# Hybrid mLSTM / gated delta-net step: weight splits scheduled ahead, and small vector work moved to GpSimd

## The chip, the cores and the metric

The kernel runs on one core of a Trainium2 chip. The metric is the device time of one execution in microseconds, from the first instruction to the last; the figure for a kernel is the median of its runs. A profiled execution gives the trace that everything below is read from.

## The reference

One inference step of a two-layer trunk on 512 prompt tokens and 8 x 4 decode tokens, all 544 handled as columns of one activation matrix of 1024 rows. Layer 0 mixes tokens with an mLSTM, layer 1 with a gated delta rule (the delta-net); each is followed by a squared-ReLU MLP of width 4096, and each sub-layer by a layer norm. The part that the change touches is the delta-net. Cut to what matters:

```
proj = x @ w_in                                  # q, k, v, z, b, a
c = silu(causal depthwise conv of width 4 over qkv, state conv0 in front)
q, k = l2norm per head;  beta = sigmoid(b);  g = -exp(a_log) * softplus(a + dt_bias)
# per token, in exact chunked form for the prompt:
S_t = e^{g_t} S_{t-1} + beta_t k_t (v_t - e^{g_t} S_{t-1}^T k_t)^T ;   o_t = S_t^T q_t
y = (head_rms(o) * norm_w * silu(z)) @ w_out
# outputs also hold the new S (8 samples x 16 heads of 128 x 128) and the last 3 conv rows
```

All matrices are fp32. A product is made from three fp32r products (high x high, low x high, high x low), so each weight tile has to be split into a high and a low part on the chip before TensorE can use it.

## The kernel before

**Weights.** Every weight is a tile of 128 x 8 x 128 values, 512 KB. `load_w` (L172) takes one of two `wraw` buffers, issues the load on SP's queue (L177), takes a buffer for the high part `wh` and one for the low part `wl` (two of each), and calls `split` (L109): ScalarE (ACT) rounds the raw tile to `wh` (L110), VectorE (DVE) writes `wl` = raw - `wh` (L111). `mm3` (L186) then issues 24 products of 272 columns on TensorE (PE) for one half of the tokens (L191), so 48 for a weight.

**Order.** The kernel is written in the Tile framework. Each engine's instructions stand in one queue, executed in order; the framework decides that order ahead of time, taking among the instructions that its plan finds ready the one that was written first. `tc.high_priority(offset=n)` makes the instructions of a block count as if written n instructions earlier. On the chip an instruction whose input is late holds everything behind it in its engine's queue.

**Delta-net (L913 on).** `ORDER` (L57) is the list of steps: `p` = `project(u)` for eight units of two heads (four weights each: k, q, v, v), `y` = `gate_out(g)` for four groups (four weights each), `w` = `out(g)` (four weights each). Between them three lanes advance in small steps: after every three products `mm3` calls `tick`, and each lane takes a step every 3 to 6 ticks (`PERIODS`, L58). The first lane holds `prepare` and `invert` (the triangular inverse of a unit's 128 x 128 chunks), the second `scan` (the chunk recurrence of the prompt), the third `decode` and `update` (the 8 x 4 decode tokens, and their states). `finish` (L165) runs the rest of a lane's work where a later step needs it.

- `conv` (L978) builds `pre` for one weight's channels: three zeros in front (L982), the conv state of the 8 samples (L983), and the projection out of PSUM (ACT, L984 to L986); copies the last rows to `cvo` for output (L988, L989); then `acc`, four taps (ACT L993, DVE L995), a sigmoid (DVE L507, ACT L508 to L510) and the product (L999, and for the samples L1002 and L1007).
- `project` copies the samples' k or q for the second head of the pair (L1033).
- `invert` uses GpSimd (POOL) for a memset and a few block copies: L1148, L1150 (scales the inverse of the 16 x 16 blocks, once it has come back through DRAM as `xc`), L1176 to L1178.
- `update` (L1403): for each of the two halves of the samples it masks the tokens' values with DVE (`VM`, L1411, two of 128 x 512), then for each of four heads fetches the state tile `st` of four samples (`sst`, four buffers, loaded three ahead by `states`), scales the keys on ACT (`KM`, L1416), issues three products of 512 columns into PSUM `pS` (L1419), and for each of the four samples DVE does state x decay + `pS` (L1424, 128 x 128). The new state is stored (L1425).

PSUM has three banks of tag g, two of a, two of s and one of t; the lanes' small products use s and a.

Of the kernel before, what the change touches and what calls it, by code (L numbers as in the profile page):

```python
# [25 lines left out]
NCH = TP // P  # L26
# [44 lines left out]
def hybrid_kernel(  # L71
# [26 lines left out]
    V, S, G, T = nc.vector, nc.scalar, nc.gpsimd, nc.tensor  # L98
    dma = nc.sync.dma_start
# [59 lines left out]
    lanes, done = [], set()  # L159
# [98 lines left out]
    bmask = cp.tile([P, NB], F32, name="bmask")  # L258
# [6 lines left out]
    with tc.tile_pool(name="tmpc", bufs=1) as tp:  # L265
# [45 lines left out]
        for i in lvl:  # L311
            w = 2 << i
# [234 lines left out]
    with tc.tile_pool(name="mc", bufs=1, reuse_waits="tile") as mc, ExitStack() as mx:  # L547
# [9 lines left out]
        with tc.tile_pool(name="mg", bufs=1, reuse_waits="tile") as mg:  # L557
# [29 lines left out]
            b = gt("b", "sp_u")  # L587
# [315 lines left out]
    with tc.tile_pool(name="gc", bufs=1, reuse_waits="tile") as gc, ExitStack() as gx:  # L903
# [63 lines left out]
        W = 3 + TP + 7 * NB  # L967
        WC = W - 3
        def samp(t):
            return t[:, 3 + TP:W].rearrange("p (b t) -> p b t", t=7)  # L970

        def tl(name, tag=None, bufs=1, n=4, dt=F32):
            return gp.tile([P, n, P], dt, tag=tag or name, name=name, bufs=bufs)

        def cv(name, n):
            return gl.tile([P, n], F32, tag="cv", name=name, bufs=NCV)

        def conv(ct, cvt, slot, dp, ds, pss):  # L978


            pre = cv("pre", W)
            V.memset(pre[:, 0:3], 0.0)  # L982
            V.tensor_copy(samp(pre)[:, :, 0:3], cvt[:, slot])  # L983
            S.copy(pre[:, 3:3 + HN], pss[0])  # L984
            S.copy(pre[:, 3 + HN:3 + TP], pss[1][:, :TP - HN])
            S.copy(samp(pre)[:, :, 3:7], pss[1][:, TP - HN:HN].rearrange("p (b t) -> p b t", t=TS))  # L986
            cvo = gp.tile([P, 27], F32, tag="cvo", name="cvo", bufs=2)
            V.tensor_copy(cvo[:, 0:3], pre[:, TP:TP + 3])  # L988
            V.tensor_copy(cvo[:, 3:27].rearrange("p (b t) -> p b t", t=3), samp(pre)[:, :, 4:7])  # L989
            dma(o_conv[:, ct, :], cvo)  # L990
            acc = cv("acc", WC)
            cw = [cst[:, C_CW + 4 * ct + q:C_CW + 4 * ct + q + 1] for q in range(4)]
            S.activation(acc, pre[:, 0:WC], AF.Copy, scale=cw[0])  # L993
            for q in range(1, 4):
                V.scalar_tensor_tensor(acc, pre[:, q:q + WC], cw[q], acc, op0=ALU.mult, op1=ALU.add)  # L995
            sgm = pre[:, 0:WC]
            sigmoid_chain(sgm, acc)
            dp = acc[:, 0:TP] if dp is None else dp
            V.tensor_tensor(dp, acc[:, 0:TP], sgm[:, 0:TP], op=ALU.mult)  # L999

            a3, s3 = acc[:, TP + 3:WC], sgm[:, TP + 3:WC]
            V.tensor_tensor(  # L1002
                ds[:, 0:7],
                a3[:, 0:49].rearrange("p (b t) -> p b t", t=7)[:, :, 0:4],
                s3[:, 0:49].rearrange("p (b t) -> p b t", t=7)[:, :, 0:4],
                op=ALU.mult)
            V.tensor_tensor(ds[:, 7], a3[:, 49:53], s3[:, 49:53], op=ALU.mult)  # L1007
            return dp, pre[:, 0:TP]

        def spare():  # L1010
# [2 lines left out]
        def project(u):  # L1013

            g, base, ct = u // 2, 12 * (u // 2) + 4 * (u % 2), 4 * u
            st = {"u": u}
            cvt = gp.tile([P, 4, NB, 3], F32, tag="cvt", name="cvt", bufs=2)
# [11 lines left out]
            for w in range(2):  # L1029
                pss = first.pop(0) if first else proj(wb[base + w])  # L1030
                xs = kqx[:, w, j0].rearrange("p (b t) -> p b t", t=TS)
                dst, sq = conv(ct + w, cvt, w, kq[:, w], xs, pss)
                V.tensor_copy(kqx[:, w, j0 + 1], kqx[:, w, j0])  # L1033
                pt = mtile("t")
                if w == 0:
                    for ch in range(NCH):
                        T.transpose(pt[:, ch * P:(ch + 1) * P], dst[:, ch * P:(ch + 1) * P], ident)
                    S.copy(ktok, pt.rearrange("p (c d) -> p c d", c=NCH))
                    for ch in range(NCH):
                        sq = gp.tile([P, P], BF16, tag="k_sq", name="k_sq", bufs=1)  # L1040
# [362 lines left out]
        def update(g, ua, ub):  # L1403

            khl, vhl = (r32(t) for t in ua["dec"])
            sts = states(g, [(h, q) for q in range(2) for h in range(4)])
            for q in range(2):
                VM = []
                for w in range(2):
                    VM.append(tl("VM", ("tok", "sx")[w], dt=F32R))  # L1410
                    V.tensor_tensor(VM[w], vhl[:, w:w + 1].to_broadcast([P, 4, P]),  # L1411
                                    bmask[:, 4 * q:4 * q + 4].unsqueeze(2).to_broadcast([P, 4, P]), op=ALU.mult)
                for h in range(4):
                    st = next(sts)
                    KM = tl("KM", ("kqs", "UAs")[h % 2], n=2, dt=F32R)
                    S.activation(KM, khl, AF.Copy, scale=blk[:, h:h + 1])  # L1416
                    pS = mtile("s").rearrange("p (b d) -> p b d", b=4)
                    for i, (a, b) in enumerate(((0, 0), (0, 1), (1, 0))):
                        T.matmul(pS, lhsT=KM[:, a], rhs=VM[b], start=(i == 0), stop=(i == 2))  # L1419
                    glc = (ua if h < 2 else ub)["glc"][:, h % 2]  # L1420
                    for r in range(4):
                        bb = 4 * q + r
                        t = st[:, r]
                        V.scalar_tensor_tensor(t, t, glc[:, NCH + bb:NCH + bb + 1], pS[:, r], op0=ALU.mult, op1=ALU.add)  # L1424
                    dma(o_ss[g, :, h, 4 * q:4 * q + 4], st)  # L1425
                    yield

# [213 lines left out]
```

## Time and profile before

| | us |
|---|---|
| median of 3 runs | 1831.82 |
| lowest and highest of the runs | 1825.68, 1838.59 |
| the profiled execution | 1825.97 |
| its span, first to last instruction | 1824.3 |
| DVE busy, of the span | 1060.5 (58%) |
| ACT busy | 827.4 (45%) |
| GpSimd busy | 55.1 (3%) |

Times in the rows are counted from the span's start. A busy PE is a modelled figure: a product's duration overlaps the next one's, so the pace of the products is read from their starts. The delta-net runs from about 710 to 1420 us.

### The profile page before, as it was taken

To read this page: it belongs to the slowest core of one execution; us is meant where nothing else is said; L and a number is where in the kernel's file an instruction comes from. 1 tells how busy PE (TensorE), PEld (TensorE's weight loads), DVE (VectorE), ACT (ScalarE), POOL (GpSimd) and SP (SyncE) were. 2 spreads that over 40 slices of the span, in tenths; PEclk is the share of its full clock that TensorE was granted. 3 is DMA by queue.
4 is the path that set the end of the run, shared out by engine and by line. 5 is a ranking of instruction groups with operands and counts; after the bars stand their busy time and mean duration, and the time that the engine had idled before them with its cause. 6 is when DMAs were issued, how large, how long until landed. Compare 5 with 4: busy or idle time off the path is not lost.

```text
span 1824.3 us, 35692 instructions
## 1 busy us (share of the span) xinstructions
PE 1755.2 (96%) x14580; PEld 1687.1 (92%) x14580; DVE 1060.5 (58%) x2648; ACT 827.4 (45%) x1874; POOL 55.1 (3%) x105
## 2 busy tenths in 40 slices
PE   7999999999999998999899999999999999999997
PEld 7999998999999998889779989998898999999996
DVE  6564767432244368776855877685578643234436
ACT  5444346331234147675643664574346542124314
POOL 2000000000000000011001000000100000000000
PEclk9999999999999999898978999997799999999998
DMA  4122222222223222223314423431232222222311
GB/s 160 58 105 64 71 93 93 71 92 87 88 93 105 82 74 61 56 50 98 111 55 122 123 68 103 130 90 41 79 121 90 90 85 93 82 93 86 111 60 50
DMA packets 84293, 158.88 MB, mean 87 GB/s; under 512 B 37537, under 2 KB 41505, under 8 KB 83617
## 3 DMA queue, kind: packets, MB, share of 16 engines
q1 hardware_dynamic: 84128, 156.60, 27.6%
q8 instruction: 115, 1.88, 0.4%
q14 instruction: 50, 0.40, 0.1%
HBM read 140.51 MB, written 16.06 MB: 86 GB/s over the span
## 4 chain that ended last, share of the span: by engine, by line
PE 81%; DVE 10%; ACT 5%; DMA 2%; issue 1%; POOL 0%; SPq 0%; ACTq 0%; DVEq 0%; POOLq 0%
PE pg_t L191 40%; PE pm_s L191 12%; PE pm_a L191 12%; PE pm_s L1368 2%; DVE lnt L377 1%; DVE lnt L378 1%; PE pm_s L1419 1%; PE pm_s L1254 1%; PE pm_a L1090 1%; PE pm_s L1265 1%; DVE acc L995 1%; ACT wh L110 1%; DVE wl L111 1%; DVE XL L389 1%; PE pm_s L1281 1%
## 5 line engine op out<-in xcount | busy, mean ns | idle before, releaser
L111 DVE TENSOR_TENSOR wl<-wraw,wh 128x1024 fp32r<-128x1024 f32 x200 | 244.7, 1224 | 360.9 <-ACT wh L110 360.3
L191 PE MATMUL pg_t<-XH,wh 128*128 128x272 f32 x1480 | 446.0, 301 | 8.7 <-ACT XH L110 7.6
L191 PE MATMUL pg_t<-XH,wl 128*128 128x272 f32 x1480 | 438.4, 297 | 7.5 <-DVE wl L111 7.5
L191 PE MATMUL pg_t<-XL,wh 128*128 128x272 f32 x1480 | 439.3, 297 | 0.1
L110 ACT CAST wh<-wraw 128x1024 fp32r<-128x1024 f32 (+1 forms) x201 | 210.4, 1047 | 465.4 <-PE pg_t L191 212.4
L191 PEld LDWEIGHTS pg_t<-XH,wh 128*128 128x128 f32 x1480 | 285.3, 193 | 13.0 <-ACT XH L110 7.6
L191 PEld LDWEIGHTS pg_t<-XH,wl 128*128 128x128 f32 x1480 | 284.5, 192 | 10.0 <-DVE wl L111 8.9
L191 PEld LDWEIGHTS pg_t<-XL,wh 128*128 128x128 f32 x1480 | 284.9, 193 | 2.4 <-DVE XL L111 0.4
L191 PE MATMUL pg_t<-h,wh 128*128 128x272 f32 x672 | 129.2, 289 | 0.0
L191 PEld LDWEIGHTS pg_t<-h,wh 128*128 128x128 f32 x672 | 105.6, 188 | 0.3
L191 PE MATMUL pg_t<-h,wl 128*128 128x272 f32 x336 | 96.9, 288 | 0.0
L191 PE MATMUL pm_a<-h,wh 128*128 128x272 f32 x496 | 95.3, 288 | 0.0
L191 PE MATMUL pm_s<-h,wh 128*128 128x272 f32 x496 | 94.9, 288 | 0.0
L191 PE MATMUL pm_s<-XH,wh 128*128 128x272 f32 x288 | 84.1, 292 | 0.0
L191 PE MATMUL pm_s<-XH,wl 128*128 128x272 f32 x288 | 83.7, 291 | 0.0
L393 DVE SCALAR_TENSOR_TENSOR XR<-XR,pg_t 128x272 f32<-128x272 f32 x118 | 51.1, 434 | 56.1 <-PE pg_t L191 55.4
L191 PE MATMUL pm_s<-XL,wh 128*128 128x272 f32 x288 | 83.7, 291 | 0.0
L191 PE MATMUL pm_a<-XL,wh 128*128 128x272 f32 x280 | 82.4, 294 | 0.9 <-DVE XL L389 0.8
L191 PE MATMUL pm_a<-XH,wh 128*128 128x272 f32 x280 | 82.9, 296 | 0.0
L191 PE MATMUL pm_a<-XH,wl 128*128 128x272 f32 x280 | 81.5, 291 | 0.0
L191 PEld LDWEIGHTS pm_s<-h,wh 128*128 128x128 f32 x496 | 77.9, 188 | 0.2
L191 PEld LDWEIGHTS pm_a<-h,wh 128*128 128x128 f32 x496 | 78.0, 188 | 0.1
(573 smaller groups left out, 3924.6 us busy)
## 6 DMA issues: line engine op xcount, KB each, us to landing
wraw<-in_w SPq DMA_DIRECT2D x64, 512.0 KB, 3.5
wraw<-in_wb SPq DMA_DIRECT2D x48, 512.0 KB, 3.5
wraw<-in_w2a SPq DMA_DIRECT2D x32, 512.0 KB, 3.5
sst<-in_s SPq DMA_DIRECT2D x64, 256.0 KB, 3.0
wraw<-in_wa SPq DMA_DIRECT2D x24, 512.0 KB, 3.5
wraw<-in_w2b SPq DMA_DIRECT2D x24, 512.0 KB, 3.4
out_ss<-sst SPq DMA_DIRECT2D x32, 256.0 KB, 3.0
wraw<-in_wbo SPq DMA_DIRECT2D x16, 512.0 KB, 3.8
```

Source lines behind the costliest of these rows:

```text
L110: S.copy(hi, src)
L111: V.tensor_tensor(lo, src, r32(hi), op=ALU.subtract)
L191: T.matmul(ps, lhsT=wt[:, k, :], rhs=xt[k][:, HS[h]], start=first and k == 0 and q == 0, stop=last and k == n - 1 and q == 2,)
L377: V.tensor_tensor(t, x, rs, op=ALU.mult)
L378: V.tensor_tensor(t, t, mu, op=ALU.subtract)
L389: V.tensor_tensor(XL[j][:, HS[h]], x, r32(XH[j][:, HS[h]]), op=ALU.subtract)
L393: V.scalar_tensor_tensor(x, x, ALPHA if first else 1.0, ps, op0=ALU.mult, op1=ALU.add)
L995: V.scalar_tensor_tensor(acc, pre[:, q:q + WC], cw[q], acc, op0=ALU.mult, op1=ALU.add)
L1090: T.matmul(pk[:, q * 256:(q + 1) * 256], lhsT=kq[:, 0, c0:c0 + P], rhs=kq[:, :, c0:c0 + P], start=True, stop=True)
L1254: T.matmul(pks[:, w], lhsT=kq[:, w, cc], rhs=St, start=True, stop=True)
L1265: T.matmul(pv[:, j], lhsT=X[:, 4 * (ch // 2) + 2 * j + ch % 2], rhs=rhs[:, j] if ch else vtok[:, j, 0], start=True, stop=True)
L1368: T.matmul(pkq[:, r], lhsT=t[:, r], rhs=kqf[:, :, o:o + 4], start=True, stop=True)
```

## The change

1. `load_w`: the load and the split of a weight stand in a block of high priority, with an offset of 300 while the lanes run (the delta-net) and 0 elsewhere; the `wh` and `wl` buffers are taken before the load is issued and not after.
2. `conv`: the two small writes to `pre` and the two to `cvo` go from DVE to GpSimd. `acc` is made as wide as `pre`, so that the samples' product is one instruction of 32 columns and not two (28 and 4). `project`: the copy of the second head goes to GpSimd.
3. `update`: the mask of the values goes from two DVE instructions of 128 x 512 to eight GpSimd instructions of 128 x 128 per half; the state is scaled by four GpSimd instructions of 128 x 128, before the products; DVE then adds `pS` to the four samples' states in one instruction of 128 x 512. After the first scaling of each half the lane gives way once more (`yield`).

```
+AHEAD = 300
 def load_w(src, alloc=None):
     raw = pool.tile([P, KD, P], F32, tag="wraw", name="wraw", bufs=WBUFS[0])
-    dma(raw, src)
     ... (wh, wl are taken here)
-    split(wh, wl, raw)
+    with tc.high_priority(offset=AHEAD if lanes else 0):
+        dma(raw, src)
+        split(wh, wl, raw)
 def conv(...):
-    V.memset(pre[:, 0:3], 0.0)
-    V.tensor_copy(samp(pre)[:, :, 0:3], cvt[:, slot])
+    G.memset(pre[:, 0:3], 0.0)
+    G.tensor_copy(samp(pre)[:, :, 0:3], cvt[:, slot])
...
-    V.tensor_copy(cvo[:, 0:3], pre[:, TP:TP + 3])
-    V.tensor_copy(cvo[:, 3:27].rearrange("p (b t) -> p b t", t=3), samp(pre)[:, :, 4:7])
+    G.tensor_copy(cvo[:, 0:3], pre[:, TP:TP + 3])
+    G.tensor_copy(cvo[:, 3:27].rearrange("p (b t) -> p b t", t=3), samp(pre)[:, :, 4:7])
...
-    a3, s3 = acc[:, TP + 3:WC], sgm[:, TP + 3:WC]
-    V.tensor_tensor(ds[:, 0:7], a3[:, 0:49]..., s3[:, 0:49]..., op=ALU.mult)
-    V.tensor_tensor(ds[:, 7], a3[:, 49:53], s3[:, 49:53], op=ALU.mult)
+    a3, s3 = (t[:, TP + 3:W].rearrange("p (b t) -> p b t", t=7)[:, :, 0:4] for t in (accw, pre))
+    V.tensor_tensor(ds, a3, s3, op=ALU.mult)
 def project(u):
-    V.tensor_copy(kqx[:, w, j0 + 1], kqx[:, w, j0])
+    G.tensor_copy(kqx[:, w, j0 + 1], kqx[:, w, j0])
 def update(g, ua, ub):
-    V.tensor_tensor(VM[w], vhl[:, w:w + 1].to_broadcast([P, 4, P]), bmask[...].to_broadcast([P, 4, P]), op=ALU.mult)
+    for r in range(4):
+        G.tensor_scalar(VM[w][:, r], vhl[:, w], bmask[:, 4 * q + r:4 * q + r + 1], None, op0=ALU.mult)
     for h in range(4):
         st = next(sts)
+        glc = (ua if h < 2 else ub)["glc"][:, h % 2]
+        for r in range(4):
+            bb = NCH + 4 * q + r
+            G.tensor_scalar(st[:, r], st[:, r], glc[:, bb:bb + 1], None, op0=ALU.mult)
+        if h == 0:
+            yield
...
-        for r in range(4):
-            V.scalar_tensor_tensor(t, t, glc[:, NCH + bb:NCH + bb + 1], pS[:, r], op0=ALU.mult, op1=ALU.add)
+        V.tensor_tensor(st, st, pS, op=ALU.add)
```

## Rows read from the trace of the kernel before

**Rows 1.** The page's busy time of three engines, share of the span, instructions.
```profile
PE 1755.2 (96%) x14580; PEld 1687.1 (92%) x14580; DVE 1060.5 (58%) x2648; ACT 827.4 (45%) x1874; POOL 55.1 (3%) x105
```

**Rows 2.** Busy time by stretches: length, engines (instructions), granted PE clock, DMA share, GB/s.
```profile
820.00:840.00 20.00, 18.38 (x132) 17.76 (x130) 14.60 (x61) 9.50 (x32) 0.95 (x1) 0.89 0.34 106
840.00:860.00 20.00, 20.00 (x269) 19.26 (x268) 12.35 (x39) 10.83 (x30) 4.14 (x6) 0.77 0.35 97
900.00:920.00 20.00, 13.26 (x202) 10.23 (x201) 14.33 (x48) 7.89 (x19) 3.56 (x8) 0.76 0.59 187
920.00:940.00 20.00, 19.08 (x140) 16.13 (x140) 4.77 (x13) 7.87 (x23) 0.00 (x0) 0.64 0.00 1
1140.00:1160.00 20.00, 18.59 (x335) 16.90 (x335) 10.90 (x29) 8.96 (x23) 3.56 (x8) 1.00 0.21 65
1240.00:1260.00 20.00, 17.52 (x277) 15.01 (x276) 6.70 (x17) 8.11 (x16) 3.57 (x8) 0.63 0.14 34
1280.00:1300.00 20.00, 16.59 (x102) 15.16 (x101) 15.19 (x55) 9.50 (x27) 0.00 (x0) 0.82 0.27 78
1300.00:1320.00 20.00, 19.82 (x249) 18.90 (x251) 8.06 (x29) 2.68 (x5) 2.23 (x5) 0.67 0.35 99
```

**Rows 3.** PE's waits, 700 to 1440 us: total us, times, longest.
```profile
PE pg_t L191 <- DVE wl L111: 7.1, 4, 3.4
PE pm_t L1062 <- DVE acc L999: 3.8, 3, 2.2
PE pm_s L1243 <- DVE tb L1125: 3.5, 2, 2.8
```

**Rows 4.** PE's timeline: start us, us, line, what, [idle before].
```profile
880.25 0.29 PE L191 MATMUL pg_t<-XH,wh 128*128 128x272 f32 x1
880.38 0.28 PE L191 MATMUL pg_t<-XL,wh 128*128 128x272 f32 x1
...
910.89 0.60 PE L191 MATMUL pg_t<-XH,wl 128*128 128x272 f32 x1 [3.37 <-DVE wl L111]
...
911.74 0.43 PE L191 MATMUL pg_t<-XH,wl 128*128 128x272 f32 x1
911.97 0.43 PE L191 MATMUL pg_t<-XH,wh 128*128 128x272 f32 x1
```

**Rows 5.** Timelines of ACT and DVE ahead of that wait.
```profile
900.96 1.05 ACT L110 CAST wh<-wraw 128x1024 fp32r<-128x1024 f32 x1
...
906.12 2.57 DVE L1424 SCALAR_TENSOR_TENSOR sst<-sst,glc,pm_s 128x128 f32<-128x128 f32 x9
...
909.63 2.34 DVE L111 TENSOR_TENSOR wl<-wraw,wh 128x1024 fp32r<-128x1024 f32 x2
```

**Rows 6.** DVE's groups, whole run: xcount, busy us, mean ns, idle before.
```profile
L111 DVE TENSOR_TENSOR wl<-wraw,wh 128x1024 fp32r<-128x1024 f32 x200 | 244.7, 1224 | 360.9 <-ACT wh L110 360.3
L1424 DVE SCALAR_TENSOR_TENSOR sst<-sst,glc,pm_s 128x128 f32<-128x128 f32 x128 | 36.8, 341 | 9.5 <-PE pm_s L1419 9.3
...
L1063 DVE TENSOR_TENSOR vtokb<-pm_t,scl 128x512 f32<-128x512 f32 x16 | 10.9, 684 | 2.3 <-PE pm_t L1062 2.2
L1411 DVE TENSOR_TENSOR VM<-vhl,bmask 128x512 fp32r<-128x512 f32 x16 | 10.9, 690 | 0.1
L983 DVE COPY pre<-cvt 128x24 f32<-128x24 f32 x32 | 5.6, 177 | 0.0
```

**Rows 7.** Timelines of POOL and DVE, two stretches: the nearest GpSimd operation.
```profile
850.61 1.92 POOL L1150 TENSOR_SCALAR DB<-xc,par 128x128 f32<-128x128 f32 x2 [23.47 <-DMA xc<-dx]
...
850.75 1.31 DVE L111 TENSOR_TENSOR wl<-wraw,wh 128x1024 fp32r<-128x1024 f32 x1
...
912.09 1.19 POOL L1150 TENSOR_SCALAR DB<-xc,par 128x128 f32<-128x128 f32 x2 [15.89 <-DMA xc<-dx]
```

**Rows 8.** The page's DMA issues: xcount, KB each, median us to landing.
```profile
sst<-in_s SPq DMA_DIRECT2D x64, 256.0 KB, 3.0
...
out_ss<-sst SPq DMA_DIRECT2D x32, 256.0 KB, 3.0
```

More of the change, by code (lines that the diff above doesn't have):

```diff
@@ L987, in conv @@
             cvo = gp.tile([P, 27], F32, tag="cvo", name="cvo", bufs=2)
-            V.tensor_copy(cvo[:, 0:3], pre[:, TP:TP + 3])
-            V.tensor_copy(cvo[:, 3:27].rearrange("p (b t) -> p b t", t=3), samp(pre)[:, :, 4:7])
+            G.tensor_copy(cvo[:, 0:3], pre[:, TP:TP + 3])
+            G.tensor_copy(cvo[:, 3:27].rearrange("p (b t) -> p b t", t=3), samp(pre)[:, :, 4:7])
             dma(o_conv[:, ct, :], cvo)
-            acc = cv("acc", WC)
+            accw = cv("acc", W)
+            acc = accw[:, 0:WC]
             cw = [cst[:, C_CW + 4 * ct + q:C_CW + 4 * ct + q + 1] for q in range(4)]
@@ L999, in conv @@
             V.tensor_tensor(dp, acc[:, 0:TP], sgm[:, 0:TP], op=ALU.mult)
-            a3, s3 = acc[:, TP + 3:WC], sgm[:, TP + 3:WC]
[L1002 to L1006, printed above, removed]
-            V.tensor_tensor(ds[:, 7], a3[:, 49:53], s3[:, 49:53], op=ALU.mult)
+            a3, s3 = (t[:, TP + 3:W].rearrange("p (b t) -> p b t", t=7)[:, :, 0:4] for t in (accw, pre))
+            V.tensor_tensor(ds, a3, s3, op=ALU.mult)
             return dp, pre[:, 0:TP]
@@ L1410, in update @@
                     VM.append(tl("VM", ("tok", "sx")[w], dt=F32R))
-                    V.tensor_tensor(VM[w], vhl[:, w:w + 1].to_broadcast([P, 4, P]),
-                                    bmask[:, 4 * q:4 * q + 4].unsqueeze(2).to_broadcast([P, 4, P]), op=ALU.mult)
+                    for r in range(4):
+                        G.tensor_scalar(VM[w][:, r], vhl[:, w], bmask[:, 4 * q + r:4 * q + r + 1], None, op0=ALU.mult)
                 for h in range(4):
                     st = next(sts)
+                    glc = (ua if h < 2 else ub)["glc"][:, h % 2]
[4 more added lines that the diff above has]
+                        yield
                     KM = tl("KM", ("kqs", "UAs")[h % 2], n=2, dt=F32R)
@@ L1419, in update @@
                         T.matmul(pS, lhsT=KM[:, a], rhs=VM[b], start=(i == 0), stop=(i == 2))
-                    glc = (ua if h < 2 else ub)["glc"][:, h % 2]
-                    for r in range(4):
-                        bb = 4 * q + r
-                        t = st[:, r]
-                        V.scalar_tensor_tensor(t, t, glc[:, NCH + bb:NCH + bb + 1], pS[:, r], op0=ALU.mult, op1=ALU.add)
+                    V.tensor_tensor(st, st, pS, op=ALU.add)
                     dma(o_ss[g, :, h, 4 * q:4 * q + 4], st)
```

## The prediction

> **What bounds the kernel now.** I read the busy shares first. TensorE is busy 96% of the span, DVE 58%, GpSimd 3% [rows 1], so nothing that shortens another engine's work pays by itself: it pays only where TensorE stands still or runs at its lower clock. So I then cut the delta-net into stretches of 20 us [rows 2]. The reader should look at two columns there, PE's busy time and the granted clock. Most stretches not shown have 19 to 20 us busy at clock 1.00. The rows shown are those where this fails, and one (1140) that holds a triangular inverse and still keeps clock 1.00 with 1.41 us idle.
>
> Third, what a lower clock costs. In [rows 4] two products of 272 columns start 0.13 us apart at 880 us, and 0.23 us apart at 911 us, where the granted level is the lower one (1.2 GHz). So a microsecond at the lower level gives away (0.23 - 0.13) / 0.23 = 0.44 us. A stretch of 20 us with mean clock c spent 40 x (1 - c) us there and lost 17.6 x (1 - c).
>
> Fourth, why PE stops. Its waits [rows 3] name late weight splits (7.1 us in 4 waits), a late convolution (3.8) and DVE's small inverse steps (3.5). The longest is the clearest: PE stops, restarts at 910.89 with a product that needed `wl` [rows 4], and has the lower clock from there. ACT had made a high part at 900.96 to 902.01, but DVE did the two waiting low parts at 909.63 only; just before, it was doing nine state updates of L1424 in a row [rows 5]. That is the place the change is aimed at. A split that was ready to run stood behind small steps in an in-order queue, and PE paid twice: the idle time, and the clock behind it.
>
> **The change part by part.**
>
> *What DVE loses.* `update` now: 128 instructions of L1424 at 341 ns mean, 43.7 us if none overlapped and 36.8 us by their busy time [rows 6]. After: 32 additions of 128 x 512 with one operand in PSUM. L1063 is the same shape with one PSUM operand, 684 ns [rows 6]: 21.9 us. Saved 14.9 to 21.8; I take 18. The masks L1411, 16 x 690 ns = 10.9 us, go entirely. The small convolution instructions: 4 in each of 32 calls and 16 copies of the second head go, and 32 products merge into others, 176 instructions at no more than the 177 ns of L983 = 31 us; some have 3 elements and not 24, so I take 23. Sum 18 + 11 + 23 = 52 us of about 500 that DVE does in the delta-net.
>
> *What GpSimd gets.* 64 masks and 128 scalings of 128 x 128. The nearest row is L1150, of that size: two took 1.19 us at 912, 1.92 us at 850 [rows 7], so 0.60 to 0.96 us each, 114 to 184 us for 192. The 144 small instructions are bounded by nothing and by 0.60 us, 0 to 86 us; with a fifth of the elements or fewer I take 0.2 us, 29 us. Together some 140 to 215 us on an engine that is busy 55 us now [rows 1]: GpSimd's total stays far from being the bound, its queue in an `update` does not (below).
>
> *The merged product* reads 32 columns as one instruction; wider `acc` costs no time, as only its first 568 columns are filled, as before, and the new ones are never read. No new wait there.
>
> *The priority.* It adds no work. A split (1.05 us on ACT, 1.22 us on DVE) goes ahead of small steps, so each small step can be later by those 2.3 us at most, once per weight. A load that goes ahead on SP's queue stands before state loads there, and waits for its `wraw` buffer; a state load and store take 3.0 us each [rows 8] and are asked for three ahead, which covers it. Where the split already waits for PE to release its buffer, the priority changes nothing.
>
> *What comes back, place by place* [rows 2]. (a) 900 to 940: idle 6.74 + 0.92 = 7.7 us, clock 17.6 x (0.24 + 0.36) = 10.6, together 18.2. The same kind of work at 1140 loses 1.4, so up to 16.8 can come back, and since an inverse stands in this stretch too, I take 15. (b) 820 to 860: idle 1.6, clock 17.6 x (0.11 + 0.23) = 6.0, together 7.6. One split wait stands in it, and an inverse; half, 3.8. (c) 1240 to 1260: idle 2.5, clock 6.5, together 9.0. PE waits there for the product of a convolution that DVE does late [rows 3]; the relief of DVE helps, the priority hardly; a third, 3. (d) 1280 to 1320: idle 3.6, clock 9.0, together 12.6. PE waits behind DVE and ACT steps of a scan [rows 3], DVE is busy 15.2 of 20 us; a quarter, 3. (e) The split waits elsewhere, 7.1 - 3.4 less one in (b): 2. Sum 27 us. The bound above is all of (a) to (e) less the 1.4: about 48 us; below, nothing.
>
> *What the moved work puts on the path.* `KM` x `VM` products now wait for eight masks and DVE's addition for four scalings. Behind that addition in DVE's queue stand the next split and the inverse's steps, and PE waits for both. In the inverse, POOL's L1150 and L1176 now queue behind scalings of 0.6 to 0.96 us. `acc` on ACT waits for POOL's two writes to `pre`. The extra yield covers the first scaling and the masks with other products, and scalings of later heads can run as soon as their state has landed. I take 3 us; the bound above is the slower rival below.
>
> Net: 27 - 3 = 24 us. The profiled execution took 1825.97, so 1802. The median of the runs stands 5.85 us above that execution; I add a third, and forecast **1804 us**.
>
> **The rivals.**
>
> *Hidden anyway.* The low clock stands around inverses and decode steps, whose tiny products keep PE's records busy, and may come back whatever the splits do; DVE is not full (58%). Then only the split waits return, 7.1 us [rows 3]: 1825.97 - 7 = 1819, or 1825 with the median's offset. For it: in (c) and (d) no split is what PE waits for. Against: (a), where it plainly is.
>
> *Contention takes the gain.* At 850.61 the two POOL instructions took 1.92 us while DVE made a `wl`, at 912.09 1.19 us while it made none; that `wl` took 1.31 us and not the mean 1.22 [rows 7, 6]. If each of 192 big POOL instructions slows DVE by 0.09 us, DVE gives back 17 of its 52 us; if they exclude each other for all of 0.60 us, it gives back 115, more than it won, and splits and small steps are late again: about 1826, plus or minus 12. The rows speak for the small figure. The Trainium skill, "GPSIMD Engine Reference" (section 1, Specifications, and section 8, Key points), says that GpSimd shares its SBUF interfaces with VectorE and contends with VectorE instructions that have two SBUF inputs, and it advises VectorE for elementwise work. By that rule alone this change is wrong-headed; this case's trace agrees on the contention (1.92 against 1.19 us) and bounds it as above.
>
> *Slower: GpSimd is the pace of `update`.* Place: the start of each of the eight half updates. Masks and first scaling are 12 POOL instructions, 7.1 to 11.5 us [rows 7], against 2 x 0.69 = 1.4 us of DVE before [rows 6]. In PE's fixed order the products on `VM` stand where the plan thought them ready. If POOL runs at the slow end, PE stands up to 11.5 - 1.4 - 4 (the cover of one lane step, an estimate from the 20 us that four heads take) = 6.1 us at each, and by (a) a stop of 7.7 us brought 10.6 us of lower clock behind it, 2.4 us in all for each us of stop. It decides from the point where POOL is later than the plan by more than that step. Four of the eight stops cost 4 x 6.1 x 2.4 = 58 us, less the gain of 27: 1826 + 31 = 1857. Also the ring of four state buffers: load 3.0, four scalings 2.4 to 3.8, addition 0.7, store 3.0 = 9.1 to 10.5 us, 2.3 to 2.6 us a head. That is less than a lane step, but not by much. Against it: GpSimd is idle for long times, and the scalings are ready early.
>
> **How the numbers follow.** Forecast, a gain of 13 to 40 us (1787 to 1813): 0.46. More than that, with (b) to (d) cured too (below 1787): 0.09. Hidden anyway: 0.22, and contention: 0.10, both within 1814 to 1842. Slower, 1842 to 1890: 0.13. The range 1779 to 1842 leaves out some 0.05 below and 0.13 to 0.15 above. Within 1% of 1831.82 is 1813.5 to 1850, about what a measurement can tell from no change: faster 0.55, same 0.33, slower 0.12. The likeliest case's own range is 1787 to 1813.
>
> **What would show it.** Right: no wait of PE for `wl` L111 over 1 us in the delta-net; DVE's busy time down by about 50 us, POOL's up to 195 to 270; the 900 to 940 stretch (by its work) at clock near 1.00; PE's idle time in the delta-net down by over 10 us. Wrong: PE or DVE waiting for POOL `VM` or `sst` for more than a few us; POOL instructions of 128 x 128 nearer 1.3 than 0.6 us; DVE's means risen by more than a tenth; or the clock low around the inverses as before though no split is late.

## The result, and the profile after

The changed kernel takes **1850.64 us** (median of 4 runs, 1848.94 to 1854.34). Against the kernel before, on the same chip, the ratio is 1.011 with a 95% interval of 1.0082 to 1.0138: 1.1% slower. The forecast was 1804, with a range up to 1842: both the time and the sign were wrong. The profiled execution took 1849.81, against 1825.97 before, so 24 us have to be found. One further execution of the kernel before took 3345 us and isn't counted in its median.

The page's busy times come first (engine, us, share of the span, instructions), then stretches of the changed kernel (length; PE, PEld, DVE, ACT and POOL busy; granted PE clock; DMA share; GB/s).

```profile
PE 1764.1 (95%) x14580; PEld 1693.1 (92%) x14580; DVE 1033.4 (56%) x2360; ACT 830.8 (45%) x1874; POOL 221.8 (12%) x441
```
```profile
700.00:1440.00 740.00, 687.71 (x6226) 638.23 (x6224) 488.99 (x1292) 406.73 (x1049) 208.38 (x408) 0.91 0.29 84
...
900.00:920.00 20.00, 15.06 (x90) 13.14 (x88) 13.43 (x42) 8.64 (x20) 14.66 (x24) 0.91 0.59 187
920.00:940.00 20.00, 16.50 (x283) 14.79 (x284) 6.88 (x18) 8.05 (x15) 4.52 (x8) 0.66 0.26 78
...
980.00:1000.00 20.00, 16.14 (x236) 13.70 (x234) 7.74 (x22) 5.76 (x16) 17.87 (x31) 0.76 0.28 83
1000.00:1020.00 20.00, 19.97 (x161) 17.80 (x162) 5.82 (x10) 8.58 (x22) 9.87 (x18) 0.73 0.33 109
...
1300.00:1320.00 20.00, 16.69 (x64) 14.22 (x64) 10.55 (x47) 3.81 (x15) 0.00 (x0) 0.52 0.18 60
```

The same view of the kernel before, for the whole delta-net and the stretches that had not been interesting then:

```profile
700.00:1440.00 740.00, 703.45 (x6412) 655.48 (x6411) 534.92 (x1620) 420.72 (x1082) 40.70 (x71) 0.93 0.30 88
...
960.00:980.00 20.00, 20.00 (x138) 19.88 (x138) 9.41 (x41) 3.46 (x11) 0.61 (x1) 0.80 0.42 132
980.00:1000.00 20.00, 20.00 (x335) 17.80 (x335) 11.64 (x36) 9.64 (x24) 4.28 (x8) 0.94 0.39 116
1000.00:1020.00 20.00, 19.95 (x143) 18.83 (x142) 16.29 (x49) 10.76 (x32) 0.00 (x0) 1.00 0.53 171
```

Two things carry the loss. In these 740 us PE is idle for 52.3 us and not 36.6: 15.7 more. The mean clock is 0.91 and not 0.93, and by the prediction's measure (0.44 us lost in each us at the lower level) that is 740 x 2 x 0.02 x 0.44 = 13 us. The same two terms explain every kernel below. Over the whole span, PE's idle time (the span less PE's busy time) and the clock term (from the mean clock of the execution) come together to between 110 us (e11) and 148 us (e16), with 120 before and 147 after. What is left of the span is 1697 to 1706 us in all 20 traces.

A stretch that was nearly whole before, 980 to 1020 (clock 0.94 and 1.00), now has 3.9 us of idle time and clock 0.76 and 0.73, and GpSimd is busy for 17.87 of its first 20 us.

PE's waits, 700 to 1440 us (total, times, longest), and DVE's wait that stands behind the first:

```profile
PE pm_a L1163 <- DVE DT L1155: 10.1, 7, 3.1
PE pm_t L1036 <- DVE kq L1003: 6.5, 1, 6.5
...
PE pm_s L1424 <- POOL VM L1411: 2.2, 2, 1.6
...
PE pg_t L194 <- DVE wl L112: 0.3, 1, 0.3
```
```profile
DVE DT L1155 <- POOL DB L1149: 16.2, 7, 4.1
```

The same two waits before:

```profile
PE pm_a L1164 <- DVE DT L1156: 4.8, 5, 1.4
```
```profile
DVE DT L1156 <- POOL DB L1150: 5.8, 4, 2.5
```

The wait for the low part of a weight, 7.1 us before [rows 3], is 0.3 now: the priority does what it says. But PE now waits 10.1 us for `DT`, the transposed blocks of the inverse (4.8 before), and DVE waits 16.2 us for the GpSimd instruction that feeds them (5.8 before). The place with the longest of these waits, in time order (start, us, engine, line, what, [idle before]):

```profile
981.09 7.82 POOL L1417 TENSOR_SCALAR sst<-sst,glc 128x128 f32<-128x128 f32 x12 [15.78 <-DMA sst<-in_s]
...
981.56 0.43 SPq L1131 DMA_DIRECT2D xc<-dx  x1
...
987.17 0.28 PE L194 MATMUL pg_t<-gyh,wh 128*128 128x272 f32 x1
988.89 1.18 POOL L1149 TENSOR_SCALAR DB<-xc,par 128x128 f32<-128x128 f32 x2
990.10 0.45 DVE L1155 STREAM_TRANSPOSE DT<-DB 128x256 f32<-128x256 f32 x1 [4.13 <-POOL DB L1149]
990.47 0.31 DVE L1387 SCALAR_TENSOR_TENSOR vhl<-pm_s,scolb,vhl 128x128 fp32r<-128x128 f32 x1
990.60 1.05 PE L1163 MATMUL pm_a<-DT,U 32*32 32x16 f32 x64 [3.15 <-DVE DT L1155]
...
990.94 4.78 POOL L1411 TENSOR_SCALAR VM<-vhl,bmask 128x128 fp32r<-128x128 f32 x8 [0.88 <-DVE vhl L1387]
...
995.20 1.80 PE L1424 MATMUL pm_s<-VM,KM 128*128 128x512 f32 x3 [0.62 <-POOL VM L1411]
```

The same place before:

```profile
979.22 0.42 SPq L1132 DMA_DIRECT2D xc<-dx  x1
983.53 1.91 POOL L1150 TENSOR_SCALAR DB<-xc,par 128x128 f32<-128x128 f32 x2 [22.91 <-DMA xc<-dx]
986.74 0.44 DVE L1156 STREAM_TRANSPOSE DT<-DB 128x256 f32<-128x256 f32 x1
987.40 0.73 PE L1164 MATMUL pm_a<-DT,U 32*32 32x16 f32 x64
```

Twelve scalings, ready as soon as their states had landed, stand in GpSimd's queue ahead of `DB`. From the issue of `xc` to `DB` it takes 7.3 us and not 4.3. DVE, in order too, stands for 4.13 us at the transpose, and behind that stands `vhl`, from which GpSimd makes the masked values: so one late instruction holds three queues. PE stops for 3.15 us, and the clock is low behind it (0.76 and 0.73 above).

Where the rest lies is shown by a table over all kernels, worked out from their traces. For the same weight product in each trace, its start is compared with that in the kernel before; a column gives how much longer (+) the kernel took than before for the work that lay in that stretch of the kernel before. "DB" is the time from the issue of `xc` to `DB`, in the second and in the fourth inverse. A row is one execution; its time stands in the second column, the median in the first. The edges are the starts of weights (719, 892, 957, 1019, 1199 and 1364 us in the kernel before), and the choice of an edge can matter: with the next weight, at 902, in place of 892 the changed kernel has +15.0 and -13.2 where +7.9 and -6.1 stand.

| kernel | median | this one | DB 2nd | DB 4th | 700-900 | 900-960 | 960-1020 | 1020-1200 | 1200-1370 |
|---|---|---|---|---|---|---|---|---|---|
| before | 1831.8 | 1826.0 | 3.3 | 4.3 | 0 | 0 | 0 | 0 | 0 |
| priority only (e1) | 1825.7 | 1829.8 | 4.5 | 4.2 | -14.3 | +4.4 | -3.4 | +0.7 | +10.8 |
| convolution only (e2) | 1832.0 | 1823.3 | 3.1 | 3.3 | -1.5 | -4.6 | -2.5 | +3.9 | +3.0 |
| `update` only (e3) | 1847.1 | 1833.6 | 3.4 | 5.2 | +1.2 | -1.0 | +13.6 | +2.3 | -7.7 |
| after without priority (e4) | 1848.8 | 1842.6 | 6.9 | 7.3 | +4.1 | -4.8 | +11.8 | +5.5 | +1.2 |
| masks only (e5) | 1843.2 | 1848.0 | 3.3 | 8.4 | +0.6 | -0.3 | +7.6 | +0.1 | +13.0 |
| scalings only (e6) | 1839.6 | 1842.9 | 3.4 | 6.7 | +5.0 | -2.1 | +8.8 | +5.7 | +2.1 |
| **after** | 1850.6 | 1849.8 | 7.5 | 7.3 | +7.9 | -6.1 | +9.4 | +5.1 | +11.1 |
| after, `DB` on ACT (e7) | 1830.6 | 1833.5 | 3.8 | 4.9 | -8.3 | +4.6 | +1.5 | +4.2 | +5.7 |
| after, scalings on ACT (e8) | 1835.1 | 1847.7 | 2.5 | 11.1 | +11.2 | -12.1 | +8.2 | +8.3 | +5.8 |
| after, 2nd order (e16) | 1863.0 | 1851.6 | 6.7 | 7.3 | -1.0 | -0.2 | +11.5 | +4.8 | +9.6 |
| e16, `DB` on ACT (e17) | 1836.0 | 1840.4 | 3.7 | 4.9 | -7.7 | +2.6 | +9.0 | +4.3 | +4.7 |
| priority, conv., `DB` on ACT (e11) | 1811.7 | 1814.7 | 4.0 | 4.8 | -9.3 | +1.0 | -2.0 | +0.5 | -3.3 |
| e11, 2nd order (e15) | 1833.0 | 1832.7 | 7.4 | 5.0 | -11.5 | +6.4 | -3.5 | +10.8 | +0.5 |
| e11, 3rd order (e18) | 1828.0 | 1825.6 | 3.9 | 4.5 | -6.6 | +5.4 | -3.8 | +2.1 | -2.6 |

### The profile page after: what moved, and what is told of

Same layout as the page of the kernel before. It is cut to its first block, busy times and chain, and to the rows that moved or that the text cites. A ratio compares the mean times of both kernels' runs of the same rounds, so it can differ in the third digit from the quotient of the medians.

```text
span 1847.9 us, 35864 instructions
## 1 busy us (share of the span) xinstructions
PE 1764.1 (95%) x14580; PEld 1693.1 (92%) x14580; DVE 1033.4 (56%) x2360; ACT 830.8 (45%) x1874; POOL 221.8 (12%) x441
## 4 chain that ended last, share of the span: by engine, by line
PE 79%; DVE 9%; ACT 4%; DMA 3%; POOL 3%; issue 2%; SPq 0%; ACTq 0%; DVEq 0%; POOLq 0%
PE pg_t L194 38%; PE pm_s L194 12%; PE pm_a L194 12%; PE pm_s L1367 2%; POOL sst L1417 1%; PE pm_s L1424 1%; DVE lnt L380 1%; DVE lnt L381 1%; PE pm_a L1089 1%; PE pm_s L1253 1%; PE pm_s L1264 1%; PE pm_s L1271 1%; ACT wh L111 1%; DVE wl L112 1%; DVE XL L392 1%
## 5 line engine op out<-in xcount | busy, mean ns | idle before, releaser
L112 DVE TENSOR_TENSOR wl<-wraw,wh 128x1024 fp32r<-128x1024 f32 x200 | 245.1, 1225 | 368.6 <-ACT wh L111 367.1
L1417 POOL TENSOR_SCALAR sst<-sst,glc 128x128 f32<-128x128 f32 x128 | 82.3, 659 | 153.5 <-DMA sst<-in_s 115.6
L999 DVE SCALAR_TENSOR_TENSOR acc<-pre,cst,acc 128x568 f32<-128x568 f32 x96 | 76.8, 804 | 6.5 <-ACT acc L997 5.1
```

The costliest lines, as they stand in the source:

```text
L1417: G.tensor_scalar(st[:, r], st[:, r], glc[:, bb:bb + 1], None, op0=ALU.mult)
```

## The experiments

The theory, from the trace above: bursts of GpSimd work stand in its in-order queue ahead of the inverse's `DB`, and PE pays with stops and with the clock behind them. The rivals: the priority costs more than it brings; GpSimd and DVE contend for SBUF; the extra `yield` spoils the interleaving; any change of the order moves the time as much.

### One part alone

The weight loads' priority alone, the convolution part alone, the `update` part alone, all but the priority, and the extra `yield` alone. The experiments ran in five batches, each beside 19 to 27 executions of the kernel before, so across batches the ratios are the fairer comparison.

```diff
 # e1
+    with tc.high_priority(offset=AHEAD if lanes else 0):
+        dma(raw, src)
+        split(wh, wl, raw)
 # e2
-    V.tensor_copy(cvo[:, 0:3], pre[:, TP:TP + 3])
+    G.tensor_copy(cvo[:, 0:3], pre[:, TP:TP + 3])
...
 # e3
+    G.tensor_scalar(VM[w][:, r], vhl[:, w], bmask[...], None, op0=ALU.mult)
+    G.tensor_scalar(st[:, r], st[:, r], glc[...], None, op0=ALU.mult)
+    V.tensor_tensor(st, st, pS, op=ALU.add)
...
 # e4: the lines of e2 and e3
 # e12
+    if h == 0:
+        yield
```

> Only the priority of the weight splits (part 1 of the change); everything on the engines of before. Theory A (the update's scalings on GpSimd are what costs: 12 of them ran in a row at 981 us and held the inverse up): the priority by itself is good or neutral, 1815 to 1832 us, PE's wait for wl under 1 us. Rival B (the priority is what costs: two splits went ahead of a convolution at 749 us and PE then stood 6.5 us): 1838 to 1850 us, with a wait of several us of PE for kq. Rival D (the order is only shuffled, each variant's stalls fall anew): anywhere within 1815 to 1850.

> Only the convolution's small writes and copies on GpSimd and the merged sample product (part 2). Theory A: neutral, 1825 to 1838 us; DVE busy down by 15 to 25 us. Rival C (contention of GpSimd with DVE): slower, 1838 to 1850 us, with conv's acc waiting for GpSimd's writes to pre by several us in all.

> Only the update's masks and scalings on GpSimd, the merged addition and the extra yield (part 3). Theory A: slower than before, 1840 to 1855 us, DVE's DT waiting for GpSimd's DB for 10 us or more in all, half clock behind one of these waits. Rival B: no slower than before, 1815 to 1835 us.

> The changed kernel without the priority (parts 2 and 3). Theory A: as slow as after, 1842 to 1858 us. Rival B: 1820 to 1838 us, the waits for wl are back but the kq wait of 6.5 us is gone. Rival D: anything between.

> The kernel before with only the extra lane step in each half of the update; no work changes its engine. Theory A: no cost, 1825 to 1836 us, DB at the fourth inverse within 5 us of the issue of its xc. Rival E2 (it is the extra step that costs, as it is in every slow variant): 1838 to 1850 us.

Measured, as ratios to the kernel before: e1 0.9956 [0.993, 0.9983]; e2 1.0021 [0.9992, 1.0051]; e3 1.0082 [1.0052, 1.0112]; e4 1.0096 [1.0062, 1.013]; e12 0.9968 [0.9941, 0.9995]. So the `update` part carries the loss, and neither priority nor `yield`, each in the one order tried here, costs anything by itself. The three parts alone add up to +0.6%, the whole has +1.1%, and the priority, worth 0.44% alone (0.2% by the medians), is worth nothing measurable on top of the other parts (1.0096 without it, 1.011 with it). Two local expectations were missed: in e2 DVE's busy time fell by 9.2 us and not by 15 to 25, and in e3 DVE waited 7.8 us for `DB` and not 10 or more. A caution on the table: the profiled execution was below its median in e3 (by 13.5 us), e16 (11.4) and e2 (8.7), and above it in e8 (12.6), so these rows show less or more than the usual loss.

### The queue in front of the inverse

In e7 the two instructions of `DB` go from GpSimd to ScalarE, in the changed kernel; e9 is the same edit in the kernel before; in e8 the 128 scalings of the changed kernel go to ScalarE and the rest stays.

```diff
 # e7 (in after), e9 (in before)
-    G.tensor_scalar(DB[:, :, 16 * q:16 * q + 16], xc, par[:, q:q + 1], None, op0=ALU.mult)
+    S.activation(DB[:, :, 16 * q:16 * q + 16], xc, AF.Copy, scale=par[:, q:q + 1])
 # e8 (in after)
-    G.tensor_scalar(st[:, r], st[:, r], glc[:, bb:bb + 1], None, op0=ALU.mult)
+    S.activation(st[:, r], st[:, r], AF.Copy, scale=glc[:, bb:bb + 1])
```

> The changed kernel whole, but the inverse's first GpSimd step (DB, two instructions per inverse) is done by ACT, so it can't stand behind scalings. Theory A: the 10 to 15 us that the stretch 960 to 1020 lost come back: 1830 to 1842 us, and PE's wait for DT falls under 5 us. Rival F (it is not the queue but GpSimd's time shared with DVE, or the order of the update's steps): no change, 1845 to 1855 us.

> Control for the run with DB on ACT: the kernel before, with only the inverse's DB on ACT. Theory A (bursts on GpSimd stood in front of DB): nothing to win where GpSimd is idle, 1822 to 1834 us. Rival G (DB on ACT is simply faster, burst or not): 1805 to 1818 us, the same 20 us as there.

> The changed kernel whole, but the states are scaled by ACT and not by GpSimd; masks, convolution copies and priority as changed. Theory A: below before, 1815 to 1835 us, as the inverse no longer waits on GpSimd and ACT has the room (45% busy). Rival F: the update's products and additions are as late with ACT, 1840 us or more.

e7: 1830.64 us, ratio 1.0001 [0.9977, 1.0026], 20 us below the changed kernel, though GpSimd is still busy 213 us. e9: 1827.16 us, 0.9964 [0.994, 0.9987], 4 us below its batch's runs of before (1831.37), 7 by the ratio. Where only the priority is added, the same edit gives 6 us (e10 below, 1819.43, against e1, 1825.71). So ScalarE is worth some 4 to 7 us for `DB` where no burst stands on GpSimd, and 13 to 16 of the 20 us are left for the queue. PE's wait for `DT` at L1163 falls from 10.1 us to 1.2, but in these two traces what comes back is nearly all clock: over the whole span PE's idle time goes from 83.8 us to 82.6 only, and the clock term from 63 to 52.

In the table 700-900 goes from +7.9 to -8.3 and 960-1020 from +9.4 to +1.5, which are the stretches of the two inverses whose `DB` was late. This is not the whole account: 900-960 gives 10.7 us back, and 5.4 of the gain stand in 1200-1370. Nor does a stretch by itself measure a queue. In e9, which isn't in the table, no burst stood in front of the fourth `DB` (4.6 us after `xc`), and yet 960-1020 is 10.1 us shorter than before, against 5.5 and 7.5 us more in 700-900 and 1020-1200. What GpSimd did ahead of the second inverse in the changed kernel:

```profile
849.57 0.69 POOL L991 COPY cvo<-pre 128x3 f32<-128x3 f32 x1 [7.49 <-DMA out_conv<-cvo]
850.25 5.29 POOL L1417 TENSOR_SCALAR sst<-sst,glc 128x128 f32<-128x128 f32 x8
...
855.66 1.18 POOL L1149 TENSOR_SCALAR DB<-xc,par 128x128 f32<-128x128 f32 x2
```

`xc` had been issued at 848.2. This is the likeliest answer, but not a shown one, to where the priority's gain went: e1 is 14.3 us ahead in 700-900, e7 is 8.3 ahead, and the changed kernel, late at this inverse, is 7.9 behind. It isn't a law, though: in e15 (below) `DB` comes 7.4 us after `xc` here, on ScalarE, and the stretch is 11.5 us ahead all the same.

e8: 1835.14 us, ratio 1.004 [1.0006, 1.0075]. Taking away the scalings helps (15 us below the changed kernel) but not wholly. The eight masks alone still stand ahead of the fourth `DB`, and they start only 5.7 us after the issue of `xc`, so `DB` comes 11.1 us after it:

```profile
988.55 5.39 POOL L1411 TENSOR_SCALAR VM<-vhl,bmask 128x128 fp32r<-128x128 f32 x8 [25.14 <-PE pg_t L194]
993.92 1.17 POOL L1149 TENSOR_SCALAR DB<-xc,par 128x128 f32<-128x128 f32 x2
```

### Masks or scalings

e5 gives only the masks to GpSimd, e6 only the scalings (with DVE's one addition per head), both with the extra `yield`, both from the kernel before.

```diff
 # e5
-    V.tensor_tensor(VM[w], ...)
+    for r in range(4):
+        G.tensor_scalar(VM[w][:, r], vhl[:, w], bmask[...], None, op0=ALU.mult)
 # e6
+        G.tensor_scalar(st[:, r], st[:, r], glc[...], None, op0=ALU.mult)
-        V.scalar_tensor_tensor(t, t, glc[...], pS[:, r], op0=ALU.mult, op1=ALU.add)
+    V.tensor_tensor(st, st, pS, op=ALU.add)
```

> Of part 3 only the masks on GpSimd and the extra yield; scaling and addition stay one DVE instruction for each sample, as before. Theory A (the scalings in GpSimd's queue hold the inverse up): no cost, 1822 to 1836 us, and the inverse's DB starts within 5 us of the issue of its xc. Rival E (late masks, or the extra lane step, are what costs): 1840 to 1852 us, PE waiting for VM for 4 us or more.

> Of part 3 only the scalings on GpSimd, with the merged addition and the yield; masks on DVE as before. Theory A: the whole cost of part 3, 1838 to 1852 us, with DB of an inverse 7 us behind its xc where scalings stand in front of it. Rival E: 1822 to 1836 us.

e5: 1843.16 us, 1.0063 [1.0035, 1.0092]. e6: 1839.56 us, 1.0049 [1.0025, 1.0072]. The theory as it stood then, scalings alone, is refuted by e5: the masks alone make `DB` late too. Either half by itself is slower, and both lose at the same place: the fourth `DB` comes 8.4 us after `xc` in e5 and 6.7 in e6, and 960-1020 grows by 7.6 and 8.8. That is not all of e5's loss, since 13.0 us more stand in 1200-1370, without a known cause. In e5:

```profile
981.91 5.40 POOL L1412 TENSOR_SCALAR VM<-vhl,bmask 128x128 fp32r<-128x128 f32 x8 [20.24 <-DVE vhl L1388]
987.29 1.18 POOL L1150 TENSOR_SCALAR DB<-xc,par 128x128 f32<-128x128 f32 x2
988.50 0.45 DVE L1156 STREAM_TRANSPOSE DT<-DB 128x256 f32<-128x256 f32 x1 [3.40 <-POOL DB L1150]
...
989.00 0.73 PE L1164 MATMUL pm_a<-DT,U 32*32 32x16 f32 x64 [3.24 <-DVE DT L1156]
```

### Parts put together without the queue

With `DB` on ScalarE: the priority (e10); priority and convolution (e11); the same and the scalings on GpSimd (e13), or the masks (e14). The lines are those of e1, e2, e7, e6 and e5.

```diff
+    with tc.high_priority(offset=AHEAD if lanes else 0):
...
+    S.activation(DB[:, :, 16 * q:16 * q + 16], xc, AF.Copy, scale=par[:, q:q + 1])
```

> Priority of the splits and DB on ACT, nothing else moved. Theory A: as the priority alone, 1818 to 1828 us. Rival G: 1800 to 1812 us.

> Priority, convolution copies on GpSimd and DB on ACT; the update as before. Theory A: 1815 to 1830 us, what the parts gave alone. Rival H (the copies on GpSimd stand late in front of the convolution once splits go first, PE's wait of 6.5 us for kq): 1832 to 1845 us.

> Priority, convolution copies and the copy of the inverse on ScalarE (the version of 1811.7 us), and on top of it the scalings on GpSimd with their merged addition; masks stay on VectorE. The queue on GpSimd in front of the inverse is gone in this kernel. Queue theory: the scalings alone then cost little, 1808 to 1820 us. Rival (GpSimd's finish times at the starts of the half-updates are the price of what is left): 1818 to 1832 us if the scalings carry the 19 us between the two kernels with the copy on ScalarE (1830.6 and 1811.7).

> As the version of 1811.7 us, with only the masks of the products on GpSimd; scalings stay on VectorE. Queue theory: 1808 to 1820 us. If the masks carry the 19 us, 1820 to 1832 us, and TensorE then shows waits for the masked products on GpSimd where the half-updates start.

e10: 1819.43 us, 0.9922 [0.9895, 0.9948]. e11: 1811.65 us, 0.9876 [0.9838, 0.9915], faster than both kernels and than the 1815 to 1830 expected. e13: 1828.58, 0.998 [0.9962, 0.9998]; e14: 1835.65, 1.0022 [0.9997, 1.0048]. So `update`'s work on GpSimd seems to cost 17 to 24 us even where `DB` doesn't stand behind it, against what the queue theory expected. The next experiment shows why this can't be read so.

### Another order of the same work

Only the size of the priority is changed. No engine gets other work, but the planned order is another one.

```diff
 # e15, e16, e17
-AHEAD = 300
+AHEAD = 200
 # e18
-AHEAD = 300
+AHEAD = 450
```

> The version of 1811.7 us with another size of the priority (200 in place of 300): no engine gets other work, only the order is another one. Whatever this moves is what a mere change of order is worth. Queue theory: within 8 us of 1811.7. Rival (where the clock's low stretches fall decides, and any change of order moves them): 1820 us or more is possible, or 1803 or less.

> The version of 1811.7 us with the priority at 450: the same work on the same engines in a third order. If the 1833 us of the second order were due to the smaller priority, 1805 to 1817 us here; if any change of order moves the time by some 20 us, 1820 to 1835.

> The changed kernel with the priority at 200 in place of 300: the same work on the same engines in another order. Queue theory: still above 1838 us, as GpSimd's queue in front of the inverse is the same. Rival (the loss is an accident of one order): 1830 us or less.

> The changed kernel in the second order (priority at 200) with the copy of the inverse on ScalarE. Queue theory: the stretch from 960 to 1020 us, 11.5 us longer than in the kernel before in that order, comes back to within 4 us of it, the one from 800 to 900 gains some 5 to 10 us more, and the whole is 12 to 25 us below 1863: 1838 to 1851. Rival (the 20 us that this edit gave in the first order were an accident of the order): 1856 us or more.

The work of e11 took 1811.65 us at 300, 1833.04 at 200 (e15, ratio 1.003 [1.0, 1.0061]) and 1828.03 at 450 (e18, 0.9997 [0.9975, 1.0019]). So an order is worth up to 21 us by the medians and 28 by the ratios, 1811.65 is the lucky one of three, and the 17 to 24 us of e13 and e14 prove nothing about masks or scalings: both are within 3 us of one of the other two orders. By the same measure the single parts, of which each has one order here, carry an uncertainty that their intervals don't show.

The main theory was therefore tried in a second order. The changed kernel at 200 (e16) took 1863.0 us, 1.0172 [1.0111, 1.0233], with the same queue at the fourth inverse (7.3 us). With `DB` on ScalarE (e17) it took 1835.97, 1.003 [1.0002, 1.0058]: 27 us less, somewhat more than the 12 to 25 expected, as it was 20 at 300. PE's wait for `DT` at L1163 falls from 11.8 us to 3.2. The two traces are only 11 us apart (1851.6 and 1840.4), so most of the 27 can't be placed. The local expectation fell, however: 960-1020 was to come back to within 4 us, and is still 9.0 longer. There the masked values themselves are late:

```profile
978.20 9.90 POOL L1417 TENSOR_SCALAR sst<-sst,glc 128x128 f32<-128x128 f32 x15 [15.55 <-DMA sst<-in_s]
...
985.21 0.73 PE L1163 MATMUL pm_a<-DT,U 32*32 32x16 f32 x64
...
988.08 2.35 POOL L1411 TENSOR_SCALAR VM<-vhl,bmask 128x128 fp32r<-128x128 f32 x4
...
990.48 0.50 PE L1424 MATMUL pm_s<-VM,KM 128*128 128x512 f32 x1 [2.80 <-POOL VM L1411]
...
993.38 1.22 PE L1424 MATMUL pm_s<-VM,KM 128*128 128x512 f32 x2 [2.40 <-POOL VM L1411]
```

The inverse is in time now, but the masks stand behind 15 scalings, and PE stops twice for them. e3 stopped here for `VM` too (2.3 us, and 0.6 for `DT`). In the table's column 960-1020 the kernels part at this place. Eight have +7.6 to +13.6, and in all of these PE stops here for 2.9 to 5.8 us, for `DT`, for `VM` or for both. All those that leave `update` on DVE have 0 or less. e13 and e14, not in the table, have -1.2 and +3.4. The length of the stop doesn't settle the loss, however: e7 stops for 2.9 us in all, as e3 does, but its clock in 980 to 1000 and 1000 to 1020 is 0.91 and 1.00, against 0.67 and 0.55 in e3, and it loses 1.5 us against 13.6.

Taken together: the one edit, `DB` to ScalarE, gave 20 and 27 us in the two orders with `update` on GpSimd, and 4 and 6 us in the two kernels without. That speaks for the queue, but it isn't a proof of the size, since a mere change of order can move the time as much (21 us). What the traces show by themselves is the chain from the burst to the late `DB`, the late `DT` and PE's stop.

## Why the prediction was wrong, point by point

**What bounds the kernel: right.** PE's stops and the clock behind them decided every one of these runs: what is left of the span without them stays within 9 us in all 20 traces, while the spans differ by up to 37. From e11 to the changed kernel the profiled time differs by 35 us while DVE is busier in the faster one (1050.1 us against 1033.4).

**The step that failed: what the moved work puts on the path.** The prediction saw the mechanism ("In the inverse, POOL's L1150 and L1176 now queue behind scalings") and put 3 us on it together with all other moved work. For the queue in front of `DB` alone the runs give some 13 to 16 us in one order and 20 to 23 in the other: the 20 and 27 us of e7 and e17, less the 4 to 7 that the same edit gives without a burst (e9, e10). With what an order is worth here these sizes are rough. The prediction reasoned with GpSimd's total (idle for long times) and with one scaling of 0.6 to 0.96 us in front; but the scalings become ready together, as states land in a ring of four, so 8, 12 or 15 stand in front, 5 to 10 us. The instruction behind them is one for which PE had waited even before (4.8 us for `DT` in 5 waits). The price of a stop was less far off here: the rival's 2.4 us for each us of stop would give 7.6 us for the 3.15 at 987, and the stretch grew by 9.4. It is no rule, as e3 and e7 show.

**Place (a), 900 to 940: wrong.** Of 18.2 us, 15 were to come back. After, these 40 us have 8.4 us of idle time and clocks of 0.91 and 0.66, 17.6 x (0.09 + 0.34) = 7.6: together 16.0, so some 2 came back there, 6.1 by the table's 900-960 (whose edge matters, see above). The split wait went, and others stand in its place: in 890 to 945 PE waits for `sgmz` (1.9), `go_on` (1.7), `VM` (1.6), `DT` (1.3) and `Eh` (1.3). With the priority alone (e1) it is the same without any work moved to GpSimd, and the longest wait is for `DT`:

```profile
900.00:920.00 20.00, 12.13 (x178) 9.98 (x177) 15.56 (x57) 7.20 (x17) 1.19 (x2) 0.77 0.69 211
920.00:940.00 20.00, 15.91 (x155) 13.26 (x149) 5.29 (x16) 7.00 (x21) 2.35 (x6) 0.64 0.00 1
```
```profile
PE pm_a L1167 <- DVE DT L1159: 4.8, 1, 4.8
```

Removing the last wait of a stretch brought forth the second to last. The prediction took the whole loss of the stretch as the price of one wait, without asking what is late next. Of its own signs of being wrong, the last one came: the clock is low there as before, though no split is late (PE's wait for `wl` is 0.3 us after and 0.5 in e1).

**Places (b) to (e).** By e1, the priority alone gained 14.3 us in 700-900 (3.8 were put on (b)) and gave 10.8 back in 1200-1370 ((c) and (d) were to bring 6). The 27 us hoped for were some 3 us for the priority alone by the medians (1825.71 against 1828.95) and 8 by its ratio (0.0044 of 1829). The first loss after the change, 6.5 us of PE's waiting for `kq` at 760 us, was not foreseen; e11 has the same wait and is still 9.3 us ahead by 900. For 1200-1370 no cause is shown. The row of 1300 to 1320 above has the lowest clock of the delta-net, 0.52, with GpSimd idle, and the runs do not part there by any single edit.

**What DVE loses: mis-sized.** 52 us were forecast, 27.1 measured (1060.5 to 1033.4): 9.2 of the 23 for the small instructions (e2), 17.4 of the 29 for `update` (e3). The durations were right (the addition took 685 ns, forecast from 684). The mistake was to add up means: 177 ns is what a small copy lasts, but it overlaps its neighbours (before, L1002 and L1007 started 0.10 us apart at 742.88), so the 176 freed 52 ns each. It did not matter, since DVE was not the bound.

**What GpSimd gets: right.** 195 to 270 us forecast, 221.8 measured. The groups of the changed kernel (count, busy us, mean ns, idle before):

```profile
L1417 POOL TENSOR_SCALAR sst<-sst,glc 128x128 f32<-128x128 f32 x128 | 82.3, 659 | 153.5 <-DMA sst<-in_s 115.6 <-DVE vd L1266 15.2 <-PE pm_s L1367 10.3
L1411 POOL TENSOR_SCALAR VM<-vhl,bmask 128x128 fp32r<-128x128 f32 x64 | 41.6, 670 | 20.7 <-PE pm_s L1390 17.0 <-PE pm_s L1424 2.6 <-DVE vhl L1387 0.9
L991 POOL COPY cvo<-pre 128x3 f32<-128x3 f32 x32 | 18.2, 570 | 139.1 <-ACT pre L988 87.6 <-issue 43.8 <-DMA out_conv<-cvo 7.5
```

**The rivals.** *Hidden anyway* had no term for what the moved work costs, so it did not decide the time. For the priority alone it came nearest: it put 7 us on it, against 3 to 8 measured, and the clock around the inverse at 900 to 940 stays low (0.77 and 0.64 in e1) with no split late, as it said. That may be luck in the size, since e1's trace gains and loses over 10 us in other stretches. *Contention takes the gain*: not on DVE's side, since `wl` lasts 1225 ns after and 1224 before; on GpSimd's side it is there (last section), but the big GpSimd instructions last 659 and 670 ns on the mean, near the 0.6 us forecast. *Slower*, with 0.13, named the right engine, the right stretch (the start of a half update) and 1857 us against 1850.6, but the wrong instruction: not `VM` first (2.2 us of waits) but the inverse's `DB` (10.1, by way of `DT`). `VM` came second, once `DB` was out of the way (4.5 us in e7, 5.8 in e17). That its 1857 is near the measured time is luck: it was built from four stops of 6.1 us for `VM`. The chance was too small because that rival was tied to PE's wait for `VM` alone, while the queue had a second customer with less slack, which had been priced separately at next to nothing.

**Still open:** how the cost of masks and scalings divides where no inverse waits, the loss in 1200-1370 (11.1 of the 27.4 us that the table's row of the changed kernel adds up to), and why an order is worth up to 21 us. The prediction's range had no term for that last one.

## What to carry to other kernels

Before moving work to an idle engine, list what that engine already does on the critical path and count how much of the new work can become ready at once in front of it: the price is the burst's length at that instruction, not the engine's busy share. When a wait is removed, look up the next late instruction of the same stretch before crediting the stretch's whole loss. And where engines run a fixed planned order, run the same work in two or three orders before a difference of 1% is put down to an edit.

## What the runs showed of the hardware

A GpSimd copy of 3 elements a partition has a mean of 570 ns, longer than one of 24 (346). It is not the copy. In the changed kernel:

```profile
749.50 1.23 DVE L112 TENSOR_TENSOR wl<-wraw,wh 128x1024 fp32r<-128x1024 f32 x1 [2.28 <-ACT wh L111]
749.79 0.98 POOL L991 COPY cvo<-pre 128x3 f32<-128x3 f32 x1 [8.94 <-ACT pre L988]
750.72 0.20 POOL L992 COPY cvo<-pre 128x24 f32<-128x24 f32 x1
750.79 1.23 DVE L112 TENSOR_TENSOR wl<-wraw,wh 128x1024 fp32r<-128x1024 f32 x1
750.90 1.19 POOL L986 COPY pre<-cvt 128x24 f32<-128x24 f32 x1
...
761.87 0.19 POOL L991 COPY cvo<-pre 128x3 f32<-128x3 f32 x1 [0.58 <-ACT pre L988]
...
1150.52 0.60 POOL L1417 TENSOR_SCALAR sst<-sst,glc 128x128 f32<-128x128 f32 x1
1150.75 1.23 DVE L112 TENSOR_TENSOR wl<-wraw,wh 128x1024 fp32r<-128x1024 f32 x1 [0.39 <-ACT wh L111]
```

With DVE free of `wl` the copy took 0.19 us. The one that began 0.29 us into a `wl` took 0.98 and ended at 750.77, 0.04 us after that `wl` (750.73). The one that began at 750.90, 0.11 us into the second `wl`, took 1.19 and ended at 752.09, 0.07 us after it (752.02). Of the 16 copies of 3 elements that begin within a `wl`, 15 end 0.04 to 0.05 us after it. So a GpSimd copy that comes second waits until the DVE instruction is done, and pays with the rest of it. The other way round it need not be so: at 1150.75 a `wl` begins while a GpSimd scaling has 0.36 us to go, and neither lasts longer than usual (1.23 and 0.60 us). Of the 13 `wl` that begin within a GpSimd copy or scaling in this trace, one took 1.39 us and the others 1.18 to 1.24, and DVE's mean did not move.

The Trainium skill, "SBUF — State Buffer" (section "SBUF: two separate sides"), says that the port pair that DVE and GpSimd share is an exclusive lock: whichever starts first holds it for the whole instruction, and a DVE instruction with two SBUF inputs takes it against a GpSimd one that reads SBUF. The trace agrees in the first two pairs, where DVE came first, and not in the last, where GpSimd did.
